# Whole products and masked evacuations in RWKV's triangular inverse, and a planner with the trace's durations

## The chip, the cores and the metric

The kernel runs on one core of one Trainium2 chip. The metric is the device time of one execution in microseconds, the median of several runs; less is better. TensorE (PE in the profile) multiplies, with a weight load (PEld) ahead of each product; VectorE (DVE), ScalarE (ACT) and GpSimd (POOL) do the elementwise work; SyncE (SP) issues the transfers.

## What is computed

One layer of a streaming encoder over 1024 prompt tokens and 32 tokens of a sample, width 1024, in float32. After an RMS norm a combined projection feeds two mixers side by side, four HGRN2 heads of 128 and eight RWKV-7 heads of 64; then come an output projection, cross attention to 256 memory rows and a SwiGLU block with 2816 hidden features.

```python
def layer(x, mk, mv, hg_s0, rw_s0, shift0, lb, lw):
    n = rmsnorm(x, lw['norm_mix'])
    p = n @ lw['w_in']
    hg_o, hg_s = hgrn2_mixer(p[..., :HG_COLS], lb, lw['hgrn_norm'], hg_s0)
    rw_o, rw_s, rw_shift = rwkv7_mixer(p[..., HG_COLS:], shift0, rw_s0, ...)
    x = x + jnp.concatenate([hg_o, rw_o], axis=-1) @ lw['w_out']
    x = x + cross_attend(rmsnorm(x, lw['norm_cross']), mk, mv, lw['w_cq'], lw['w_co'])
    n = rmsnorm(x, lw['norm_ffn'])
    x = x + (jax.nn.silu(n @ lw['w_ff1']) * (n @ lw['w_ff3'])) @ lw['w_ff2']
    return x, hg_s, rw_s, rw_shift
...
    # in rwkv7_mixer, token by token
    def step(S, xs_t):
        r_t, w_t, k_t, v_t, kk_t, a_t = xs_t
        sa = jnp.einsum('bhvk,bhk->bhv', S, -kk_t)
        S = (S * w_t[:, :, None, :] + sa[..., None] * (kk_t * a_t)[:, :, None, :]
             + v_t[..., None] * k_t[:, :, None, :])
        return S, jnp.einsum('bhvk,bhk->bhv', S, r_t)
```

The kernel doesn't run RWKV's recurrence token by token. It takes chunks of 64 tokens. Within a chunk the updates depend on one another through a strictly lower triangular 64 x 64 matrix A, and the chunk is solved with the inverse of I - A.

## The kernel before

**A recorded graph and a planner.** No engine call is issued where it stands in the code. Each call becomes a node of a graph (`Graph.record`), whose edges are the reads and writes of the tiles; products that follow one another without a `cut` share a node. `Graph.order` then runs a list schedule in time: each engine has a clock and a list of ready nodes, the most urgent node that fits is taken, and each node gets a place in SBUF or a PSUM bank for as long as it needs it. Urgency is the longest path to the end, lowered by a bias: the projections carry 1e5 less, so they fill in where the mixers' chains have nothing ready. `price` gives the microseconds of a call on its engine, `wait` the delay from one engine's result to another's use, `change` what PE loses between two nodes. The order that comes out is fixed: every engine works through its queue in it, and waits on semaphores where an operand isn't there yet. So the prices set the order, not the time of any instruction. All instructions are issued at one line (L337), and the profile is read by tiles and shapes.

**Places.** SBUF is given out in units of 66 words. Tiles in "r" regions are float32r operands; "f0", "ma", "mb" hold the rest. `FIFO` limits how many tiles of a class are live and takes them in order of recording; `AHEAD` allows two RWKV units ("rw", "rc") and one HGRN2 unit at a time; `LEAD` opens a later stage when so many nodes of the earlier ones are left.

**Stages.** Phase 0 holds the projections and the mixers, phase 1 the memory's keys and values, then output projection, cross attention, feed-forward. Large products are split in a high and a low float32r part and done as three products of 352 columns each (`gemm`).

**RWKV.** `rwkv(j)` handles a pair of heads, j = 0 to 3, in five segments: four of 256 prompt tokens (four chunks, `nc_` = 4) and the sample's 32 (one chunk). Each segment calls `inverse` once, 20 times in all. `inverse` holds A - I of both heads as the two diagonal blocks of a 128 x 128 float32 tile (`abd`) per chunk, and a float16 copy of it (`a16`). It grows the inverse by blocks of 2, 4, .. 64 in five levels after a first one, and ends with a Newton step. x is the inverse found so far and y its transpose, both stacked (128 rows of both heads, 64 columns per chunk). `product(left, right)` multiplies a block-diagonal operand with a stacked one, one product of 64 columns per chunk. Since the stationary operand has to be block-diagonal, `place` copies a stacked result into the diagonal blocks of `xbd` or `pbd`, by two ScalarE copies, one for each head. A level is then: p = a16 times y, masked by VectorE; p placed in pbd; y plus the product of xbd and p, by VectorE; x plus the product of pbd and x, by VectorE; x placed in xbd. The tiles off the diagonal are set to zero once at the start, in two sets (`DIAG` = 2) that take turns.

Of the kernel before, what the change touches and what calls it, by code (L numbers as in the profile page):

```python
# [11 lines left out]
F32 = mybir.dt.float32  # L12
F32R = mybir.dt.float32r
F16 = mybir.dt.float16
# [6 lines left out]
T = TP + NS  # L21
# [5 lines left out]
LAST = [(256, 512), (768, 288), (0, 256)]    # the tokens' blocks in the last products  # L27
# [36 lines left out]
FIFO = {"wr": 2, "wh": 2, "wl": 2, "p": 44, "h": 12, "rp": 5, "wr2": 4, "wh2": 8, "wl2": 8, "ckv": 7, "mrow": 2}  # L64
# [22 lines left out]
class View:  # L87
    """A part of a tile: the indices it covers, and the steps that make the same part of the placed tile."""
# [37 lines left out]
    def free(self):  # L126
        """The indices along the free dims."""
        return (self.ix[0] & ((1 << 20) - 1)).ravel()


class Buf:
# [24 lines left out]
    def touch(self, node, view, write):  # L156
        """Edges from the earlier accesses that this one must follow."""
# [41 lines left out]

def wait(a, b):  # L200
    """us from an engine's result to another engine's use of it."""
    if a == b:
        return 0.0
    if b == "tensor":
        return 0.2 + WAIT_PE
    return {"tensor": 0.2, "gpsimd": 0.08}.get(a, 0.14) + WAIT


def price(eng, method, args, kw):
    """(us on the engine, us until its result can be used beyond that)."""  # L210
    out = args[0] if args else kw.get("out")
    n = math.prod(out.shape[1:]) if out is not None and hasattr(out, "shape") else 1
    if method == "dma_start":
        return 0.45 + n * out.shape[0] * 4 / 380e3, 1.2
    if eng == "tensor":
        if method == "transpose":
            return (0.056 if args[1].shape[0] == 64 else 0.109), 0.0
        lhs = kw["lhsT"]
        m = math.prod(lhs.shape[1:])
        if lhs.dtype == F16:  # L220
            return 0.029, 0.0
        if lhs.dtype == F32R:
            return (n if n >= 256 else 4 * n) / 2400 + 0.002, 0.0
        return (n / 790 if m == 64 else 4 * n / 2400 + 0.003), 0.0
    if eng == "vector":
        if method == "tensor_reduce":
            n = math.prod(args[1].shape[1:])
        return 0.065 + n * 1.04e-3 + (0.065 if method in ("scalar_tensor_tensor", "tensor_tensor_scan") else 0.0), 0.0
    if method == "affine_select":
        return 0.3, 0.0  # L230
    if method == "memset":
        return 0.04 + n * 0.5e-3, 0.0
# [11 lines left out]
def change(a, b):  # L244
    """us that the tensor engine loses between two nodes' products: weights that a short product doesn't hide."""
    if a is None:
        return 0.0
# [1356 lines left out]
```

## Time and profile before

| | |
|---|---|
| median of 3 runs | 2035.69 us (2035.36 to 2036.48) |
| span of the profiled execution | 2034.7 us |
| PE busy | 1954.2 us, 96% |
| DVE, ACT, POOL busy | 1101.1, 801.0, 622.5 us |
| transfers | 100.59 MB, mean 49 GB/s |

The span runs from the first to the last instruction of one execution; what lies around it makes up the rest of a run's time. PE's busy time counts a product from its start to its modelled end, and products overlap, so a busy PE isn't one at its peak. Idle time is put down to the engine whose work ended last before the waiting instruction; "issue" stands for time in which nothing that the profile shows was waited for. Tiles go by the region of SBUF that they lie in ("f", "r", "ma", "mb", "wr") or by "bank".

### The profile page before, as it was taken

The numbers are of one execution on the slowest core, as the hardware profiler recorded it, in microseconds if no ns is written. First come the engines' busy times: TensorE is split into PE (matmuls) and PEld (weight loads), VectorE is DVE, ScalarE is ACT, GpSimd is POOL, SyncE is SP. The second block draws the span as 40 slices with busy tenths as digits, with TensorE's granted clock in tenths as the row PEclk, the third lists the DMA queues.
The fourth block names the chain that finished last, engine by engine and source line by source line (L and its number), as shares of the span: only waits on it lengthen the run. The fifth ranks groups of instructions, "written<-read, shape, count | busy, mean of one in ns | idle before, by whom it ended". The sixth has DMA issues, their size and how long they took to land.

```text
span 2034.7 us, 36538 instructions
## 1 busy us (share of the span) xinstructions
PE 1954.2 (96%) x14417; PEld 1813.2 (89%) x14417; DVE 1101.1 (54%) x2584; ACT 801.0 (39%) x2066; POOL 622.5 (31%) x954
## 2 busy tenths in 40 slices
PE   7989999998999899899999999999999999999998
PEld 6878777787877788899989999999999999999997
DVE  4876677768767766635754356333333344323345
ACT  4576546845765676633332233121111112111122
POOL 4742343334434331206300056230022233310221
PEclk8999999998999999899999999999999999999999
DMA  4100100011010101541211111111211111111112
GB/s 139 42 22 25 35 23 27 23 34 33 22 32 18 33 23 58 179 147 42 73 42 42 42 53 42 42 40 40 59 50 39 40 58 42 50 40 53 46 42 86
DMA packets 159115, 100.59 MB, mean 49 GB/s; under 512 B 7776, under 2 KB 153824, under 8 KB 158944
## 3 DMA queue, kind: packets, MB, share of 16 engines
q1 hardware_dynamic: 158944, 98.26, 16.0%
q8 instruction: 113, 1.85, 0.4%
q14 instruction: 58, 0.48, 0.1%
HBM read 86.69 MB, written 11.55 MB: 48 GB/s over the span
## 4 chain that ended last, share of the span: by engine, by line
PE 59%; DVE 4%; POOL 1%; ACT 1%; issue 1%; DMA 1%; SPq 0%; DVEq 0%; ACTq 0%
PE bank L337 59%; DVE f L337 2%; ACT f L337 1%; POOL f L337 1%; DVE r L337 1%; POOL r L337 1%; DVE mb L337 0%; ACT mb L337 0%; DMA wr<-in_w_ck_dram 0%; ACT r L337 0%; DMA f<-mix_scratch 0%; DMA wr<-in_w_cq_dram 0%; DVE wr L337 0%; SPq L337 0%; POOL mb L337 0%
## 5 line engine op out<-in xcount | busy, mean ns | idle before, releaser
L337 PE MATMUL bank<-r 128*128 128x352 f32 x5904 | 1040.1, 331 | 12.4 <-POOL r L337 5.3
L337 PEld LDWEIGHTS bank<-r 128*128 128x128 f32 x5904 | 955.1, 190 | 27.6 <-POOL r L337 5.8
L337 DVE TENSOR_TENSOR f<-bank,f 128x256 f16<-128x256 f32 (+9 forms) x689 | 252.6, 391 | 355.4 <-PE bank L337 339.8
L337 PE MATMUL bank<-mb,r 128*128 128x352 f32 (+3 forms) x2448 | 411.5, 325 | 4.6 <-DVE r L337 2.5
L337 PEld LDWEIGHTS bank<-mb,r 128*128 128x128 f32 x2448 | 396.1, 188 | 9.5 <-DVE r L337 4.3
L337 POOL TENSOR_TENSOR f<-f 128x352 f32<-128x352 f32 (+6 forms) x242 | 198.2, 835 | 482.0 <-ACT f L337 459.4
L337 PE MATMUL bank<-f 128*128 128x64 f16 (+7 forms) x2612 | 291.6, 253 | 35.2 <-DVE f L337 15.7
L337 ACT CAST r<-wr 128x1024 fp32r<-128x1024 f32 (+2 forms) x154 | 145.1, 946 | 311.8 <-PE bank L337 298.1
L337 ACT ACTIVATE f<-f 128x256 f32<-128x256 f32 (+5 forms) x372 | 147.0, 411 | 245.9 <-DVE f L337 217.7
L337 PEld LDWEIGHTS bank<-f 128*128 128x128 f32 (+4 forms) x1564 | 163.6, 162 | 66.8 <-DVE f L337 16.9
L337 ACT COPY f<-f 64x256 f16<-64x256 f16 (+1 forms) x408 | 149.1, 367 | 46.1 <-DVE f L337 37.8
L337 DVE TENSOR_TENSOR r<-wr,r 128x1024 fp32r<-128x1024 f32 (+2 forms) x124 | 142.1, 1150 | 43.5 <-ACT r L337 43.3
L337 DVE TENSOR_TENSOR wr<-wr,f 128x1024 f32<-128x1024 f32 x82 | 105.8, 1292 | 104.5 <-DMA wr<-in_w_ff_dram 89.1
L337 POOL TENSOR_TENSOR r<-f,r 128x352 fp32r<-128x352 f32 x48 | 62.3, 1312 | 271.1 <-DVE f L337 216.9
L337 POOL TENSOR_SCALAR f<-f 128x64 f32<-128x64 f32 (+6 forms) x124 | 54.7, 442 | 159.2 <-DVE f L337 100.0
L337 DVE TENSOR_TENSOR ma<-bank,ma 128x352 f32<-128x352 f32 (+6 forms) x96 | 45.3, 486 | 94.6 <-PE bank L337 84.1
L337 PEld LDWEIGHTS <-f 128*128 128x128 f16 x1156 | 52.5, 99 | 35.6 <-issue 8.2
L337 POOL TENSOR_TENSOR r<-wr,r 128x1024 fp32r<-128x1024 f32 x30 | 71.7, 2393 | 29.5 <-ACT r L337 25.9
L337 ACT CAST mb<-f 128x352 fp32r<-128x352 f32 x66 | 30.9, 484 | 123.0 <-DVE f L337 114.7
L337 PE MATMUL bank<-f,mb 64*64 64x64 f32 (+7 forms) x830 | 75.3, 250 | 1.4 <-DVE f L337 1.1
L337 ACT ACTIVATE f<-bank,f 128x256 f32<-128x256 f32 (+4 forms) x122 | 51.1, 432 | 56.4 <-DVE f L337 19.7
L337 DVE TENSOR_TENSOR f<-bank,r 128x352 f32<-128x352 f32 x60 | 30.4, 518 | 77.0 <-PE bank L337 77.0
(167 smaller groups left out, 1770.6 us busy)
## 6 DMA issues: line engine op xcount, KB each, us to landing
wr<-in_w_ff_dram SPq DMA_DIRECT2D x44, 512.0 KB
wr<-in_w_in_dram SPq DMA_DIRECT2D x30, 512.0 KB
wr<-in_w_ff_dram SPq DMA_DIRECT2D x24, 384.0 KB
f<-mix_scratch SPq DMA_DIRECT2D x24, 176.0 KB
mb<-in_x_prompt_dram SPq DMA_DIRECT2D x16, 256.0 KB
wr<-in_w_ck_dram SPq DMA_DIRECT2D x8, 512.0 KB
wr<-in_w_cv_dram SPq DMA_DIRECT2D x8, 512.0 KB
wr<-in_w_out_dram SPq DMA_DIRECT2D x8, 512.0 KB
```

Source lines behind the costliest of these rows:

```text
L337: getattr(eng, method)(*args, **kw)
```

## The change

In `inverse`, the masks of the levels become block-diagonal and have the identity taken off, so that a masked product with A - I gives p + I directly. `place` is now one VectorE operation that reads the stacked product once for each half (a broadcast over the two column blocks), multiplies it by such a mask and writes all 512 columns, zeros included. With p + I in pbd, y and x need no addition: y becomes a plain product of xbd and pbd, copied from PSUM by ScalarE, and x a product of pbd and x. Where the right operand is block-diagonal too, `product_diag` takes its two column blocks in two products that accumulate. `a16`, `xbd` and `pbd` are no longer kept in sets that take turns, but are given out for each inverse; their memsets at the start are gone.

In the planner, `price`, `wait` and `change` get other constants and cases. Two classes, "raw" and "mixed", tiles of the RWKV projections, are limited to four live ones. A node's tiles are now tried largest first and all together, and small tiles keep out of the last whole page of 16 units unless the node is the oldest one. Comments are removed.

```diff
-WAIT, WAIT_PE, SWITCH = 0.0, 0.1, 0.06
+SWITCH = 0.095
...
-FIFO = {"wr": 2, ..., "ckv": 7, "mrow": 2}
+FIFO = {"wr": 2, ..., "ckv": 7, "mrow": 2, "raw": 4, "mixed": 4}
...
+WAIT = {("vector", "tensor"): 0.2, ("vector", "gpsimd"): 0.18, "vector": 0.115, ("scalar", "tensor"): 0.1,
+        ("scalar", "gpsimd"): 0.05, "scalar": 0.02, ("gpsimd", "tensor"): 0.08, "gpsimd": 0.0, "tensor": 0.21,
+        ("sync", "tensor"): 0.08, "sync": 0.0}
 def wait(a, b):
-    if a == b:
-        return 0.0
-    if b == "tensor":
-        return 0.2 + WAIT_PE
-    return {"tensor": 0.2, "gpsimd": 0.08}.get(a, 0.14) + WAIT
+    return 0.0 if a == b else WAIT.get((a, b), WAIT[a])
 def price(eng, method, args, kw):
     if method == "dma_start":
-        return 0.45 + n * out.shape[0] * 4 / 380e3, 1.2
+        return max(0.4, n * out.shape[0] * 4 / 200e3), 1.9
...
         if lhs.dtype == F16:
-            return 0.029, 0.0
+            return max(0.029, n / 2400 + 0.002), 0.0
         if lhs.dtype == F32R:
-            return (n if n >= 256 else 4 * n) / 2400 + 0.002, 0.0
-        return (n / 790 if m == 64 else 4 * n / 2400 + 0.003), 0.0
+            return (n if n >= 256 else 4 * n) * 0.4375e-3 + 0.007, 0.0
+        if k <= 64 and m <= 64:
+            return max(0.03, n * 0.92e-3), 0.0
+        if k <= 64:
+            return max(0.112, n * 1.25e-3), 0.0
+        if m <= 64:
+            return (0.059 if n >= 64 else 0.112), 0.0
+        return max(0.223, n / 600 + 0.005), 0.0
...
     if eng == "scalar":
-        return 0.095 + n * 0.83e-3 + (0.06 if any(isinstance(kw.get(k), View) for k in ("scale", "accum_out")) else 0.0), 0.0
+        pointer = any(isinstance(kw.get(k), View) for k in ("scale", "bias", "accum_out"))
+        return (0.18 if args[1].buf.space == "PS" else 0.21) + n * 0.83e-3 + (0.095 if pointer else 0.0), 0.0
...
     if method == "tensor_tensor":
-        return 0.1 + n * 2.1e-3 + (0.45 if args[3] == ALU.pow else 0.0), 0.0
+        return 0.22 + n * 2.2e-3 + (0.45 if args[3] == ALU.pow else 0.0), 0.0
...
+def cut_of_array(call):
+    method, args, kw = call
+    op = args[1] if method == "transpose" else kw["lhsT"]
+    return op.shape[0] <= 64, method != "transpose" and math.prod(op.shape[1:]) <= 64
 def change(a, b):
...
-    return 0.033 if half else SWITCH
+    return SWITCH if a is not None and cut_of_array(a.calls[-1]) != cut_of_array(b.calls[0]) else 0.0
...
+                if not first and b.kind == "F" and b.cls not in HOME and (idle == 16).sum() < 2:
+                    cand = np.where(idle[:, None] == 16, BIG, cand)
...
+                for b in sorted(sb, key=lambda b: -b.units):
+                    at = place(b, start, first)
+                    if at is None:
+                        break
...
+        both = self.both = c.tile([128, 2, 64], F32, name="both")
+        nc.vector.tensor_copy(both.rearrange("p h u -> p (h u)"), j64)
+        def diagonal(m):
+            d = c.tile([128, 2, 64], F32, name="levd")
+            nc.vector.tensor_tensor(d, m.unsqueeze(1).to_broadcast([128, 2, 64]), both, ALU.mult)
+            return d
...
-            self.lev.append(m)
+            nc.vector.tensor_tensor(m, m, self.i64, ALU.subtract)
+            self.lev.append(diagonal(m) if l else m)
...
-            self.diag.append([self.sp.tile([128, 4, 128], dt, name=n) for n, dt in (("abd", F32), ("a16", F16), ("xbd", F16), ("pbd", F16))])
-            for t in self.diag[-1]:
-                nc.gpsimd.memset(t, 0.0)
+            self.diag.append(self.sp.tile([128, 4, 128], F32, name="abd"))
+            nc.gpsimd.memset(self.diag[-1], 0.0)
...
-        abd, a16, xbd, pbd = self.diag[self.diag_n % DIAG]
+        abd = self.diag[self.diag_n % DIAG]
         self.diag_n += 1
+        a16, xbd, pbd = (self.tmp([128, 4, 128], t, F16) for t in ("a16", "xbd", "pbd"))
...
-        def place(dst, src):
-            for hf in half:
-                S.copy(dst[hf, :nc_, hf], src[hf])
+        def product_diag(left, right):
+            ps = stacked()
+            for c in range(nc_):
+                PE.matmul(ps[:, c], lhsT=left[:, c], rhs=right[:, c, 0:64], start=True, stop=False)
+                PE.matmul(ps[:, c], lhsT=left[:, c], rhs=right[:, c, 64:128], start=False, stop=True)
+            nc.cut()
+            return ps
+        def place(dst, ps, mask):
+            V.tensor_tensor(dst[:, :nc_].rearrange("p c (h u) -> p c h u", h=2),
+                            ps.unsqueeze(2).to_broadcast([128, nc_, 2, 64]),
+                            mask.unsqueeze(1).to_broadcast([128, nc_, 2, 64]), ALU.mult)
...
-        for hf in half:
-            S.copy(a16[hf, :nc_, hf], abd[hf, :nc_, hf])
-            G.tensor_tensor(x[hf], abd[hf, :nc_, hf], bc(self.lev0x[hf]), ALU.mult)
-        place(xbd, x)
+        S.copy(a16[:, :nc_], abd[:, :nc_])
+        G.tensor_tensor(xbd[:, :nc_], abd[:, :nc_], bc(self.lev0x), ALU.mult)
         V.tensor_tensor(y, product(a16, bc(self.i16)), bc(self.lev0y), ALU.mult)
         for l in range(1, 6):
-            V.tensor_tensor(p, product(a16, y), bc(self.lev[l]), ALU.mult)
-            place(pbd, p)
-            V.tensor_tensor(y32 if l == 5 else y, product(xbd, p), y, ALU.add)
-            V.tensor_tensor(x, product(pbd, x), x, ALU.add)
-            place(xbd, x)
+            place(pbd, product(a16, y), self.lev[l])
+            S.copy(y32 if l == 5 else y, product_diag(xbd, pbd))
+            ps = product(pbd, x) if l > 1 else product_diag(pbd, xbd)
+            place(xbd, ps, self.both)
+            if l < 5:
+                S.copy(x, ps)
         V.tensor_tensor(p, product(abd, y32), bc(self.i64), ALU.add)
         V.tensor_tensor(y1, product(xbd, p), y32, ALU.add)
         return y1
```

More of the change, by code (lines that the diff above doesn't have):

```diff
@@ L63 @@
 TASTE = [{"f0": 0.0, "wr": 0.0, "r0": 0.0, "mb": 20.0, "ma": 10.0}, {"f0": 20.0, "wr": 0.0, "r0": 0.0, "mb": 0.0, "ma": 10.0}]
-FIFO = {"wr": 2, "wh": 2, "wl": 2, "p": 44, "h": 12, "rp": 5, "wr2": 4, "wh2": 8, "wl2": 8, "ckv": 7, "mrow": 2}
+FIFO = {"wr": 2, "wh": 2, "wl": 2, "p": 44, "h": 12, "rp": 5, "wr2": 4, "wh2": 8, "wl2": 8, "ckv": 7, "mrow": 2, "raw": 4, "mixed": 4}
 INDEX = (np.arange(128, dtype=np.int64)[:, None] << 20) + np.arange(8 * 1056, dtype=np.int64)[None]
@@ L227, in price @@
             n = math.prod(args[1].shape[1:])
[L228 to L232, printed above, removed]
+        if method == "tensor_tensor_scan":
+            return 0.07 + n * 2.08e-3, 0.0
+        return 0.065 + n * 1.05e-3 + (0.065 if method == "scalar_tensor_tensor" else 0.0), 0.0
     if method == "preload_act_table_set":
@@ L235, in price @@
     if eng == "scalar":
-        return 0.095 + n * 0.83e-3 + (0.06 if any(isinstance(kw.get(k), View) for k in ("scale", "accum_out")) else 0.0), 0.0
+        pointer = any(isinstance(kw.get(k), View) for k in ("scale", "bias", "accum_out"))
+        return (0.18 if args[1].buf.space == "PS" else 0.21) + n * 0.83e-3 + (0.095 if pointer else 0.0), 0.0
+    if method == "affine_select":
+        return 0.35, 0.0
+    if method == "memset":
+        return 0.06 + n * 0.5e-3, 0.0
     if method == "tensor_tensor":
-        return 0.1 + n * 2.1e-3 + (0.45 if args[3] == ALU.pow else 0.0), 0.0
+        return 0.22 + n * 2.2e-3 + (0.45 if args[3] == ALU.pow else 0.0), 0.0
     if method == "tensor_scalar":
-        return 0.2 + n * (2.6e-3 if args[4] == ALU.max else 1.1e-3), 0.0
-    return 0.1 + n * 1e-3, 0.0
-def change(a, b):
-    if a is None:
-        return 0.0
-    (_, x, kx), (m, y, ky) = a.calls[-1], b.calls[0]
-    if m == "transpose":
-        full, half = y[1].dtype == F32, False
-    else:
-        full = ky["lhsT"].dtype != F16
-        half = math.prod(ky["lhsT"].shape[1:]) == 64
-    if math.prod(x[0].shape[1:]) > 64 or not full:
-        return 0.003
-    return 0.033 if half else SWITCH
+        return 0.3 + n * (2.9e-3 if args[4] == ALU.max else 1.3e-3), 0.0
+    return 0.24 + n * 1e-3, 0.0
+def cut_of_array(call):
+    method, args, kw = call
+    op = args[1] if method == "transpose" else kw["lhsT"]
+    return op.shape[0] <= 64, method != "transpose" and math.prod(op.shape[1:]) <= 64
+def change(a, b):
+    return SWITCH if a is not None and cut_of_array(a.calls[-1]) != cut_of_array(b.calls[0]) else 0.0
 class Graph:
@@ L433, in order, with place @@
         done, oldest, out = set(), 0, []
-        def place(b, start):
+        def place(b, start, first):
             units = b.units
@@ L484, in fits @@
                     return None
-                for b in sb:
-                    if b.at is None:
-                        at = place(b, start)
-                        if at is None:
-                            return None
-                        start = max(start, at[1])
+                tried = []
+                for b in sorted(sb, key=lambda b: -b.units):
+                    at = place(b, start, first)
+                    if at is None:
+                        break
+                    start = max(start, at[1])
+                    lo, hi = at[0], at[0] + b.units
+                    tried.append((lo, hi, freed[lo:hi].copy()))
+                    freed[lo:hi] = BIG
+                for lo, hi, was in reversed(tried):
+                    freed[lo:hi] = was
+                if len(tried) < len(sb):
+                    return None
             return start
@@ L499, in take @@
                     continue
-                got = place(b, start)
+                got = place(b, start, n.i == oldest)
                 assert got is not None, "no place for " + b.name
@@ L627, in constants @@
             B = 1 << l
-            m = c.tile([128, 64], F32, name=f"lev{l}")
+            m = c.tile([128, 64], F32, tag="lev0", name="lev") if l else c.tile([128, 64], F32, name="lev0y")
             G.memset(m, 0.0)
@@ L1397, in inverse @@
         half = (slice(0, 64), slice(64, 128))
-        abd, a16, xbd, pbd = self.diag[self.diag_n % DIAG]
+        abd = self.diag[self.diag_n % DIAG]
         self.diag_n += 1
+        a16, xbd, pbd = (self.tmp([128, 4, 128], t, F16) for t in ("a16", "xbd", "pbd"))
         def bc(m):
-            return m.unsqueeze(1).to_broadcast([m.shape[0], nc_, 64])
+            return m.unsqueeze(1).to_broadcast([m.shape[0], nc_, m.shape[1]])
         def stacked():
```

19 lines of the change are left out of this document (9 added, 10 removed).

## The prediction

> **What bounds the kernel now.** I read the totals of the page first, then a table of stages cut at 890 us, where the mixers and the memory's keys end and only large products are left, then who ends the waits of the weight loads before 900 us, then the granted clock around a few gaps. Columns of the stage table: the stretch, its length, then busy time and instruction count of PE, PEld, DVE, ACT and POOL, the granted clock, the DMA share and GB/s.
>
> ```profile
> span 2034.7 us, 36538 instructions
> PE 1954.2 (96%) x14417; PEld 1813.2 (89%) x14417; DVE 1101.1 (54%) x2584; ACT 801.0 (39%) x2066; POOL 622.5 (31%) x954
> core 0: 2034.7 us, clock 0.978
> ```
>
> ```profile
> 0.00:50.00 50.00, 36.17 (x210) 33.21 (x210) 19.88 (x35) 24.42 (x63) 24.10 (x74) 0.90 0.43 141
> 0.00:890.00 890.00, 823.01 (x7492) 704.46 (x7493) 607.42 (x1716) 548.17 (x1555) 338.97 (x680) 0.95 0.16 50
> 890.00:2034.70 1144.70, 1131.17 (x6927) 1108.74 (x6925) 493.65 (x868) 252.87 (x512) 283.49 (x274) 1.00 0.17 49
> 98.00:212.00 114.00, 107.58 (x1115) 90.59 (x1114) 80.00 (x236) 82.34 (x229) 41.35 (x83) 0.97 0.08 22
> 212.00:300.00 88.00, 82.95 (x662) 69.58 (x660) 59.20 (x170) 39.37 (x125) 36.80 (x74) 0.92 0.11 32
> 1255.00:2009.00 754.00, 753.97 (x4664) 751.56 (x4664) 285.52 (x439) 133.20 (x232) 169.79 (x157) 1.00 0.15 44
> 2009.00:2034.70 25.70, 17.35 (x129) 15.08 (x127) 17.14 (x32) 8.02 (x26) 8.21 (x27) 0.88 0.45 169
> ```
>
> From 890 us on PE idles 1144.7 - 1131.2 = 13.5 us, most of it in the last 26; the feed-forward stage is 4664 products in 754.0 us, 0.162 us each, without a gap. Nothing in the change touches that work. What can move lies ahead of 890: **67.0 us of PE idle** (890 - 823.0), 13.8 of them in the first 50 us, where data first arrive, and **a clock loss**: the mean clock of 0.978 is (1 - 0.978) x 2034.7 = 45 us lost, the tail at 0.88 holds 3 of it, and the rest, about 41, lies in the first 890 at 0.95. Work on PE is otherwise the bound: any product added there is paid. In the burst 98 to 212, where inverses run, ACT (72%) and DVE (70%) are about as loaded as each other; in 212 to 300, without them, ACT falls to 45%.
>
> ```profile
> PEld bank L337 <- issue: 33.6, 111, 4.5
> PEld bank L337 <- DVE f L337: 24.1, 42, 3.4
> PEld bank L337 <- ACT f L337: 9.1, 20, 2.4
> PEld bank L337 <- ACT mb L337: 9.0, 12, 2.1
> PEld bank L337 <- POOL f L337: 8.0, 5, 6.8
> PEld bank L337 <- DVE mb L337: 6.5, 12, 3.5
> PEld bank L337 <- POOL r L337: 5.8, 2, 5.3
> PEld bank L337 <- DVE ma L337: 5.3, 10, 2.2
> PEld bank L337 <- ACT ma L337: 4.3, 8, 1.3
> ```
>
> These are the waits of PE's weight loads before 900 us (total, times, longest): DVE ends 35.9 us, ACT 22.4, POOL 13.8. "Issue" is 33.6 us in 111 pieces of 0.3, PE's own pauses, which I don't count as reachable.
>
> ```profile
> 324.00:328.00 4.00, 4.00 (x34) 3.26 (x33) 2.29 (x5) 3.14 (x9) 2.68 (x3) 1.00 0.10 24
> 332.20:335.60 3.40, 2.21 (x28) 1.60 (x26) 3.30 (x8) 1.13 (x4) 2.49 (x3) 0.99 0.00 0
> 335.60:342.40 6.80, 6.75 (x36) 5.69 (x36) 3.72 (x14) 1.82 (x5) 2.09 (x4) 0.50 0.01 2
> 461.90:465.30 3.40, 1.47 (x12) 1.03 (x11) 3.33 (x7) 0.24 (x1) 1.87 (x1) 0.99 0.02 5
> 465.30:472.10 6.80, 6.80 (x24) 5.73 (x24) 3.61 (x11) 2.93 (x8) 2.36 (x6) 0.50 0.34 100
> ```
>
> So a gap is paid twice. Behind 3.4 us in which PE was busy for 2.21 or 1.47, the clock stands at 0.50 for 6.8 us, and that costs 3.4 us where PE is wanted; 41 us is about twelve such spells.
>
> **The change part by part.** The rows of the inverse, and what its new operations resemble:
>
> ```profile
> L337 ACT COPY f<-f 64x256 f16<-64x256 f16 x320 | 128.0, 402 | 37.1 <-DVE f L337 30.2 <-POOL f L337 1.4
> L337 ACT COPY f<-ma 64x256 f16<-64x256 f16 x32 | 12.9, 402 | 0.6
> L337 ACT CAST f<-mb 64x256 f16<-64x256 f32 x32 | 12.9, 403 | 30.4 <-POOL f L337 15.5 <-DVE mb L337 14.2
> L337 ACT COPY f<-f 64x64 f16<-64x64 f16 x88 | 21.1, 240 | 9.1 <-DVE f L337 7.6 <-POOL f L337 0.2
> L337 ACT COPY f<-bank 128x256 f32<-128x256 f32 x68 | 24.3, 371 | 34.0 <-PE bank L337 27.6 <-DVE mb L337 4.2 <-DVE f L337 1.3
> L337 ACT ACTIVATE mb<-mb 128x512 f32<-128x512 f32 x16 | 10.1, 634 | 3.0 <-POOL f L337 3.0
> L337 DVE TENSOR_TENSOR f<-bank,f 128x256 f16<-128x256 f32 x229 | 90.1, 418 | 32.2 <-PE bank L337 26.5 <-ACT f L337 3.6 <-ACT mb L337 0.8
> L337 DVE TENSOR_TENSOR f<-bank,f 128x64 f16<-128x64 f32 x64 | 13.2, 218 | 8.7 <-PE bank L337 7.4 <-ACT ma L337 0.9 <-issue 0.2
> L337 DVE TENSOR_TENSOR r<-bank,r 128x512 fp32r<-128x512 f32 x16 | 10.9, 691 | 14.9 <-ACT r L337 14.9
> L337 POOL TENSOR_TENSOR f<-mb,f 64x256 f16<-64x256 f32 x30 | 21.3, 709 | 31.7 <-DVE mb L337 27.1 <-PE bank L337 3.3
> L337 POOL TENSOR_TENSOR r<-wr,r 128x1024 fp32r<-128x1024 f32 x30 | 71.7, 2393 | 29.5 <-ACT r L337 25.9 <-PE bank L337 3.2
> L337 PE MATMUL bank<-f 128*128 128x64 f16 x1048 | 72.3, 195 | 9.8 <-DVE f L337 3.7 <-ACT f L337 2.6 <-ACT mb L337 2.3
> 324.93 0.18 PEld L337 LDWEIGHTS <-f 128*128 128x128 f16 x4
> 330.52 0.29 PEld L337 LDWEIGHTS <-f 128*128 128x128 f16 x8
> ```
>
> The copy counts fix the number of inverses: 352 copies of 64x256 at 22 each are 16 whole ones, 88 of 64x64 are 4 of the sample (one chunk), 68 chunks in all.
>
> *PE.* Each level's y product becomes two per chunk, and so does the first x product: 6 more per chunk, 6 x 68 = **408 more f16 products**. From a group of 4 (0.18 us) to one of 8 (0.29) each costs 0.0275 us, so 408 cost **+11.2 us**. Bounds: 0 where they fall into idle time, +28 at the 0.069 us of the whole group of such products (72.3/1048), gaps included. I take +11: PE is the bound.
>
> *ACT.* Gone are 128.0 + 12.9 + 12.9 + 21.1 = 175 us of copies. New in a whole inverse: one copy of 512 columns (0.634) and nine from PSUM (0.371), 3.97 us, 64 us for 16; the four small ones, ten copies each at under 0.24, under 10. **ACT loses about 101 us** of its 548. What hid the old copies was filler on PE; where it did not, ACT ended the wait. If the copies were behind half of ACT's 22.4 us, **-11 us**; the ends are 0 (the waits belong to other ACT work) and -22. This cover has a successor: the evacuations on DVE are late next.
>
> *DVE.* Gone: 16 x 15 evacuations of 0.418 and 4 x 15 of 0.218, 113 us. New: 16 x 10 of 512 columns at 0.691 and 4 x 10 of 128, between 0.218 and 0.418, say 0.3: 123 us. **+9 us of work**, most beside PE; at DVE's share of reachable idle (35.9 of 607) it is +1 us, all of it on the path +9. I take +1. Some dozen mask products at the start lie in the first 50 us, where DVE is busy 19.9: 0.
>
> *POOL.* 32 operations of 0.709 become 16 of 512 columns at half of 2.393, 1.2 us: -3 us, beside other work. The memsets of six tiles go as well: 0.
>
> *Latency.* In the old loop y waits for xbd, xbd for the x product and two pairs of copies: over two levels 0.42 (y) + 0.42 (p) + 0.80 + 0.42 (x) + 0.80 = 2.86 us of evacuation and three product hops. The new loop is 0.69 + 0.37 per level, 2.12 per two levels with four hops. One hop is about 0.2 (a product takes 0.195) and a hand-over. So the chain alone hardly shortens; what falls is the number of instructions that queue, seven to four per level. I count nothing beyond the ACT term.
>
> *The planner.* Before, it took 0.149 us for a 352-column product (0.162 in the row above) and 0.31 for a copy of 64x256 (0.402); now 0.161 and 0.42. A product placed by too fast prices stands in PE's queue before its operand is there, and what stands behind it waits too. Better prices should move filler ahead of it. Nothing in the trace prices this; nearest is the idle that DVE and POOL end, 35.9 + 13.8 = 49.7. A fifth gives **-10 us**; the ends are -30 and, as any new order can also hit a gap, +15. The limits of four "raw" and four "mixed" tiles, and pages kept whole, lie within these ends: 0 extra, as three live blocks cover evacuation. DMA issues are the same; SP's queue, sorted by dearer loads (2.6 against 1.8 us by the planner), is within the same ends.
>
> *The clock.* Idle would go from 67 to about 47 (13.8 of both at the start, so 53 to 33, by 38%). Of 41 us, 5 belong to the start and some to the stage's end; 38% of the 32 or so left is **-12 us**; ends 0 and -25.
>
> A rule of the Trainium skill speaks against the last term. In "TensorE: Matmul & The Clock Gate", section "Why this matters for your kernels", it asks for no PE-idle gaps of over about 3 us. By that rule, gaps of 1 us would turn no clock down, and thinning them would save no spell. Here spells came behind windows that were 65% and 43% busy (2.21 and 1.47 of 3.40), so the trace goes with the looser reading, but it does not show how much less idle is enough.
>
> Sum: +11 - 11 + 1 - 10 - 12 = **-21 us** on the span of 2034.7; the median of the runs lies 1.0 above it, so 2034.7 + 1.0 - 21 = **2015 us**.
>
> **The rivals.**
>
> *The spells stay.* The mixers' many small products leave PE lightly used whatever the order, and about as many spells come. For it: both windows above are short of PE work, not empty. Against: 324 to 328, full of the same mix, has clock 1.00. Without the clock term: 2035.7 - 9 = **2027**. The Trainium skill's rule above, on the page named there, would have it so too.
>
> *The products are paid and nothing comes back* (slower). If ACT's waits belong to other copies, and the order is as good as before, PE has 408 more products in a row that waits as before: +11 + 1, **2048**. It decides once relief and order together return less than 12 us. For it: ACT ends only 22 us of the waits, and bursts keep PE at 94% (107.58 of 114). Against: 42 of the named waits are under 3.5 us long, the size of a queue of copies.
>
> *DVE becomes late.* Each level now has two evacuations of 0.691 in one queue in place of 0.418: 200 x 0.27 = 54 us of chain. A quarter uncovered is +14, two more spells +7, products +11, **2067** without the relief. For: DVE ends most waits already. Against: its total grows by 9 us only.
>
> *The stage closes up.* Idle before 890 halves again beyond the forecast, order -25, clock -20, ACT -11: with +12, -44, **1991**. For: the burst of 98 to 212 runs at 94% already with its waits. Against: the waits that POOL ends, 13.8, have another cause.
>
> *It doesn't do what it says*: if planner limits undo the relief, it shows as the second rival.
>
> **How the numbers follow.** Chances: forecast 0.35, spells stay 0.20, paid for nothing 0.20, DVE late 0.10, closes up 0.15. The forecast's own range is 2003 to 2030. For 8 in 10 I leave out half of the DVE case and the far side of the last: 1988 to 2052. A measurement of this kernel can tell about 0.2%, 4 us, from no change. Faster than 2031.6: 0.15 + 0.34 and half or more of the second, 0.60; within: 0.12; slower: 0.28, the two slow rivals less a little.
>
> **What would show it.** ACT before 890 near 447 us; f16 products up from 17 x 68 = 1156 to 1564; DVE evacuations of 512 columns near 0.69; PE idle there near 47; mean clock near 0.984. The stage should end near 870, and everything from there on take the same 1145 us. Idle kept with ACT's waits gone and DVE's grown is the DVE rival; idle down at an unchanged clock, the first; a stage that ends past 895, the second. It is wrong altogether if the stages after it change length by more than 5 us.

## The result, and the profile after

| | before | after |
|---|---|---|
| median of the runs | 2035.91 us (2035.36 to 2036.48) | 2056.01 us (2052.03 to 2058.04) |
| span of the profiled execution | 2034.7 us | 2054.7 us |
| ACT, DVE, POOL busy | 801.0, 1101.1, 622.5 us | 691.8, 1121.6, 614.0 us |

The changed kernel is **slower by 20 us** by these medians, 0.99%; the ratio given with the result is 1.0111, 95% interval 1.0087 to 1.0135, and before took 2031.5 to 2033.7 in the later sessions, so the loss is 20 to 25 us. The forecast was 2015 us, with 2052 as the upper end of its range. The totals of the page of the changed kernel, and its core's clock:

```profile
span 2054.7 us, 36974 instructions
PE 1961.8 (95%) x14825; PEld 1822.8 (89%) x14825; DVE 1121.6 (55%) x2496; ACT 691.8 (34%) x1784; POOL 614.0 (30%) x928
core 0: 2054.7 us, clock 0.979
```

PE has the 408 products more (14825 against 14417) and is busy for 7.6 us more; it idles 92.9 us in place of 80.5; the clock is the same within 0.001. ACT has lost 109 us of work, as meant. So the work went where it should, and the time didn't follow.

**Where the time lies.** The load of the output projection's weights, `wr<-in_w_out_dram`, opens the rest of the kernel; it waits in the weights' fifo behind the loads of the memory's keys and values. Three rows of the timeline from 700 to 1000 us of each kernel give the memory's products, that first load and the mixers' last write (shortest, median and longest of one in ns, then from the first start to the last). Before:

```profile
L337 PE MATMUL bank<-r,ma x384: 275/281/561, 804.1 to 880.6; 128*128 128x256 f32 x192
L337 SPq DMA_DIRECT2D wr<-in_w_out_dram x8: 368/390/557, 873.8 to 942.3; - x8
L337 SPq DMA_DIRECT2D mix_scratch<-f x11: 319/327/349, 708.9 to 878.1; - x11
```

After:

```profile
L344 PE MATMUL bank<-r,ma x384: 277/281/557, 816.2 to 905.3; 128*128 128x256 f32 x192
L344 SPq DMA_DIRECT2D wr<-in_w_out_dram x8: 367/390/391, 899.8 to 963.6; - x8
L344 SPq DMA_DIRECT2D mix_scratch<-f x10: 319/336/356, 742.2 to 868.1; - x10
```

The mixers end 10 us **earlier** than before. But the memory's keys and values start 12 us later and end 25 later, and the load that opens the rest comes 26.0 later. The stage tables cut there (columns as in the prediction), before:

```profile
0.00:800.00 800.00, 742.00 (x6916) 628.81 (x6917) 553.30 (x1593) 492.58 (x1417) 322.95 (x644) 0.96 0.12 36
0.00:873.80 873.80, 808.90 (x7397) 691.52 (x7398) 602.05 (x1709) 541.38 (x1542) 337.44 (x678) 0.95 0.15 47
873.80:2034.70 1160.90, 1145.28 (x7021) 1121.68 (x7021) 499.02 (x875) 259.66 (x524) 285.02 (x276) 1.00 0.17 51
```

After:

```profile
0.00:800.00 800.00, 742.32 (x7268) 633.68 (x7269) 576.13 (x1494) 376.79 (x1115) 315.15 (x617) 0.96 0.12 36
0.00:890.00 890.00, 815.09 (x7762) 697.80 (x7762) 629.50 (x1627) 432.09 (x1267) 331.08 (x654) 0.95 0.15 46
0.00:899.80 899.80, 823.06 (x7811) 705.16 (x7811) 632.99 (x1629) 435.87 (x1272) 331.08 (x654) 0.95 0.16 48
899.80:2054.70 1154.90, 1138.73 (x7015) 1117.68 (x7015) 488.58 (x867) 255.96 (x513) 282.92 (x274) 1.00 0.17 50
```

Behind the load the two kernels take 1160.9 and 1154.9 us, so all of the loss is ahead of it. Of the 26.0 us there, 11.8 are more idle of PE (64.9 to 76.7) and 14.2 more busy time (808.90 to 823.06). Most of the busy time is the 408 added products, as an experiment below shows; where the 6.0 us behind the load come from wasn't traced. Up to 800 us PE idles 58.0 and 57.7 us at the same clock of 0.96: with 116 us less of ACT work there (492.58 to 376.79) its idle time is the same. From 800 us to the load PE idles 6.9 us before (73.8 - 66.9) and 19.1 after (99.8 - 80.7).

The waits of PE's weight loads before 900 us, after (the dots stand for a row of "issue" on loads that name no bank):

```profile
PEld bank L344 <- issue: 36.7, 110, 2.9
PEld bank L344 <- DVE f L344: 31.6, 47, 4.8
PEld bank L344 <- ACT f L344: 14.8, 27, 2.0
PEld bank L344 <- ACT r L344: 11.8, 9, 6.7
PEld bank L344 <- DVE r L344: 9.5, 9, 1.9
PEld bank L344 <- DVE ma L344: 7.6, 16, 1.6
PEld bank L344 <- POOL f L344: 7.1, 2, 6.7
...
PEld bank L344 <- DVE mb L344: 4.5, 10, 1.0
PEld bank L344 <- ACT mb L344: 3.1, 4, 2.0
```

The waits that ACT ends on "f" have risen from 9.1 to 14.8, those on "mb" have fallen from 9.0 to 3.1. DVE ends 31.6 us on "f" in place of 24.1. Two rows are new among the large ones: ACT r and DVE r, 21.3 us, the splits of weights. Over half of that stands ahead of the key and value products, as the group of their weight loads shows (behind the last bar the idle ahead of them, and who ended it; before, then after):

```profile
L337 PEld LDWEIGHTS bank<-r,ma 128*128 128x128 f32 x384 | 49.9, 201 | 1.7 <-DVE r L337 1.1 <-ACT r L337 0.2 <-ACT f L337 0.2
L344 PEld LDWEIGHTS bank<-r,ma 128*128 128x128 f32 x384 | 50.5, 201 | 13.6 <-DVE r L344 7.1 <-ACT r L344 4.3 <-DVE ma L344 1.7
```

How it comes about is in the chain of work that ended last (start, length, what; its part from 852 to 877 us, without the pieces of 0.02 us):

```profile
851.96 3.95 DMA wr<-in_w_ck_dram
855.95 0.04 issue
855.99 1.06 ACT r L344
857.07 1.24 DVE r L344
858.31 0.04 issue
858.35 10.06 PE bank L344 x74
868.44 0.59 ACT f L344
869.03 0.96 ACT r L344
870.00 1.24 DVE r L344
871.24 0.04 issue
871.28 5.80 PE bank L344 x47
```

A weight arrives, ACT takes its high part (1.06), DVE its low part (1.24), and PE waits for both. While the mixers run, their products can cover this, and in before, where the mixers' last write (878.1) comes with the end of these products (880.6), the same group idles 1.7 us in all. In the changed kernel the mixers have run out at 868, and the products of the keys and values go on alone to 905.

### The profile page after: what moved, and what is told of

Read it like the earlier page. It is cut to its first block, busy times and chain, and to the rows that moved or that the text cites. A ratio compares the mean times of both kernels' runs of the same rounds, so it can differ in the third digit from the quotient of the medians.

```text
span 2054.7 us, 36974 instructions
## 1 busy us (share of the span) xinstructions
PE 1961.8 (95%) x14825; PEld 1822.8 (89%) x14825; DVE 1121.6 (55%) x2496; ACT 691.8 (34%) x1784; POOL 614.0 (30%) x928
## 4 chain that ended last, share of the span: by engine, by line
PE 59%; DVE 2%; POOL 1%; ACT 1%; DMA 1%; issue 0%; DVEq 0%; SPq 0%; ACTq 0%; POOLq 0%
PE bank L344 59%; DVE f L344 2%; POOL r L344 1%; POOL f L344 1%; DVE r L344 1%; ACT r L344 0%; ACT f L344 0%; DMA wr<-in_w_out_dram 0%; DMA wr<-in_w_ck_dram 0%; DMA f<-in_mem_prompt_dram 0%; DVE ma L344 0%; ACT ma L344 0%; DVEq L1637 0%; DVE mb L344 0%; SPq L344 0%
## 5 line engine op out<-in xcount | busy, mean ns | idle before, releaser
L344 DVE TENSOR_TENSOR f<-bank,f 128x352 f32<-128x352 f32 (+9 forms) x588 | 247.5, 445 | 328.6 <-PE bank L344 315.7
L344 POOL TENSOR_TENSOR f<-f 128x352 f32<-128x352 f32 (+7 forms) x248 | 199.5, 822 | 485.7 <-ACT f L344 454.6
L344 PE MATMUL bank<-f 64*64 64x64 f32 (+8 forms) x2526 | 283.1, 259 | 45.8 <-DVE f L344 25.6
L344 ACT ACTIVATE f<-f 128x256 f32<-128x256 f32 (+6 forms) x420 | 165.1, 408 | 261.9 <-DVE f L344 218.1
L344 PEld LDWEIGHTS bank<-f 64*64 64x64 f32 (+4 forms) x1713 | 171.4, 160 | 83.7 <-DVE f L344 27.0
L344 PE MATMUL bank<-f,mb 64*64 64x64 f32 (+9 forms) x994 | 88.1, 249 | 2.7 <-DVE f L344 2.1
L344 DVE TENSOR_TENSOR ma<-bank,f 128x512 f16<-128x512 f32 (+6 forms) x135 | 65.2, 494 | 41.8 <-PE bank L344 40.7
L344 PEld LDWEIGHTS bank<-f,mb 128*64 128x64 f32 (+6 forms) x970 | 67.4, 149 | 20.2 <-issue 8.7
L344 ACT ACTIVATE f<-bank,f 128x256 f32<-128x256 f32 (+3 forms) x133 | 54.8, 428 | 81.7 <-PE bank L344 37.2
L344 ACT CAST f<-bank 128x256 f16<-128x256 f32 (+1 forms) x148 | 48.3, 338 | 80.3 <-PE bank L344 38.6
```

The source lines that it names most:

```text
L344: getattr(eng, method)(*args, **kw)
```

## The experiments

My first theory after the result, **late filler**: the instructions are as good as forecast, but the order that the planner made of them leaves the keys and values to the end. The rivals: the 408 products, the new inverse's own chain, or the new prices lose the time in any order. A third view came with the second group of runs, **the order is a draw**. All runs in one table; "load" is the first load of the output projection's weights in the profiled execution, "idle" and "clock" are PE's ahead of it. The half-memory kernels have no such entries, since their load doesn't mark the end of the same work.

| kernel | median us | ratio to before [95%] | load at | idle | clock |
|---|---|---|---|---|---|
| before | 2031.5 to 2035.9 | | 873.8 | 64.9 | 0.95 |
| after | 2056.0 | 1.0111 [1.0087, 1.0135] | 899.8 | 76.7 | 0.95 |
| inverse_only | 2064.4 | 1.0142 [1.0120, 1.0164] | 902.5 | 82.4 | 0.95 |
| planner_only | 2080.0 | 1.0226 [1.0211, 1.0241] | 919.6 | 86.0 | 0.92 |
| before_order_a | 2064.5 | 1.0153 [1.0133, 1.0173] | 902.3 | 84.7 | 0.94 |
| before_order_b | 2049.4 | 1.0082 [1.0067, 1.0097] | 888.9 | 74.0 | 0.94 |
| after_other_order | 2041.5 | 1.0045 [1.0029, 1.0061] | 880.4 | 64.2 | 0.96 |
| rows_first | 2052.4 | 1.0089 [1.0074, 1.0104] | 893.8 | 79.9 | 0.95 |
| before_rows_first | 2034.7 | 1.0013 [1.0003, 1.0023] | 869.5 | 67.7 | 0.96 |
| fewer_products | 2052.0 | 1.0098 [1.0078, 1.0119] | 895.4 | 77.7 | 0.94 |
| before_half_kv | 2013.4 | 0.9898 [0.9873, 0.9923] | | | |
| after_half_kv | 2022.0 | 0.9932 [0.9910, 0.9954] | | | |
| order_a_half_kv | 2033.1 | 1.0003 [0.9986, 1.0020] | | | |
| after_order_c | 2022.1 | 0.9946 [0.9928, 0.9965] | 864.2 | 56.6 | 0.97 |
| after_order_d | 2012.7 | 0.9897 [0.9882, 0.9912] | 855.6 | 52.9 | 0.97 |
| inverse_order_c | 2049.4 | 1.0072 [1.0057, 1.0087] | 885.6 | 67.6 | 0.96 |
| before_order_c | 2035.6 | 1.0010 [1.0000, 1.0020] | 870.3 | 63.4 | 0.97 |
| planner_order_c | 2017.6 | 0.9914 [0.9899, 0.9929] | 861.4 | 58.0 | 0.95 |
| planner_order_d | 2049.5 | 1.0072 [1.0055, 1.0089] | 890.2 | 70.3 | 0.94 |
| before_order_d | 2014.9 | 0.9913 [0.9887, 0.9939] | 857.5 | 60.5 | 0.97 |

**Each half alone.** inverse_only takes the new inverse into the planner of before:

```diff
-            V.tensor_tensor(p, product(a16, y), bc(self.lev[l]), ALU.mult)
-            place(pbd, p)
...
+            place(pbd, product(a16, y), self.lev[l])
+            S.copy(y32 if l == 5 else y, product_diag(xbd, pbd))
...
```

> The new inverse under the planner of before. Late filler (the 20 us are lost where the mixers end, because the new planner takes up the rows of the memory late, so that the products for the memory's keys and values no longer fill the mixers' last 60 us): the old planner takes them up early, so the time is near before or a little under it, 2025 to 2040. Products paid (the 408 added products are the loss): 2045 to 2056. Order worse throughout (the new prices make stalls all along the mixers): 2025 to 2040 as well, so this run doesn't tell it from late filler.

planner_only takes the new planner and keeps the old inverse:

```diff
-WAIT, WAIT_PE, SWITCH = 0.0, 0.1, 0.06
+SWITCH = 0.095
...
-            return 0.029, 0.0
+            return max(0.029, n / 2400 + 0.002), 0.0
...
```

> The old inverse under the new planner. Late filler: the memory's rows come late here too, 2050 to 2070. Products paid: 2030 to 2040, since none is added. Order worse throughout: 2050 to 2070, with PE busy less in each stretch of 100 us up to 800, not only behind it.

Measured: 2064.4 and 2080.0, both slower than the whole change (2056.0), and both above every range that was expected. The halves don't add: with the old planner the new inverse costs 29 us (by the ratio), with the new one it saves 24. The row of planner_only up to its load:

```profile
0.00:919.60 919.60, 833.61 (x7403) 711.85 (x7403) 607.66 (x1717) 547.81 (x1551) 345.20 (x680) 0.92 0.16 47
```

It does the same work as before's 7397 products there, with no instruction of another kind, 45.8 us later: 21 us more idle (86.0 against 64.9), and 24.7 us more busy time at a clock of 0.92 against 0.95. The new planner alone gave the worst order of all. (It is the prices together with the limits and the rule for places; they weren't taken apart.)

**Other orders of the same instructions.** FREE_PS and FREE_SB are the microseconds after a tile's last use at which the planner takes its PSUM bank, or its place in SBUF, for free. They are 0.2 and 0.2 in both kernels; no instruction depends on them.

```diff
-FREE_PS, FREE_SB = 0.2, 0.2
+FREE_PS, FREE_SB = 0.262, 0.14
```

> The kernel before, unchanged but for two of the planner's constants, the time after which it takes a PSUM bank and a place in SBUF for free (0.2 and 0.2 us, here 0.262 and 0.14). They change no instruction, only the order. Lost order (the order of before is a lucky draw, any other touch of the planner or the graph loses some 20 us): 2045 to 2070, with the first load of the output projection's weights later by what the time is longer. Products paid or worse prices: 2030 to 2038.

before_order_b has 0.299 and 0.278 there, and after_other_order 0.144 and 0.227 in the changed kernel:

> The same with 0.299 and 0.278. Lost order: 2045 to 2070. Products paid or worse prices: 2030 to 2038.

> The changed kernel with the same two constants at 0.144 and 0.227, the order that the planner itself holds for the best of 24 (19 us shorter by its own reckoning than the changed kernel's). Lost order: 2032 to 2045. Products paid: 2052 to 2058, since every order holds the same products.

Measured: before loses 32 and 17 us, the changed kernel gains 15, all as "lost order" has it. So a tenth of a microsecond or less in such a constant moves either kernel by about as much as the whole change did.

**The memory's rows early.** In both kernels the rows' transposes, which the keys and values need, get the highest urgency:

```diff
+        late, nc.bias = nc.bias, -BIAS
         rs = self.load_rows(...)
+        nc.bias = late
```

> The changed kernel with one edit: the loading and transposing of the memory's rows gets the highest urgency in place of the lowest, nothing else. Late filler: the first products for the memory's keys move from 816 us to under 790, the stage ends some 15 us sooner, 2035 to 2045. Products paid or order worse throughout: 2052 to 2058, unchanged.

> The kernel before with the same edit. Late filler: its first such product comes at 804 us and its idle from 790 to 890 is 9 us, so a gain of 0 to 10 us is open to it, 2026 to 2036. Products paid or order worse throughout: 2034 to 2037.

Measured: 2052.4 (from 2056.0) and 2034.7 (ratio 1.0013 [1.0003, 1.0023]). In rows_first the last of the rows is loaded at 771.0 us in place of 833.8, yet the first product for the keys starts at 821.4 in place of 816.2, where late filler had expected it under 790. The load comes 6 and 4 us earlier, and the time hardly moves. The transposes weren't what the keys and values waited for.

**The products.** The second product of each pair is left out, with the order held: the node keeps its price and its reads.

```diff
-                PE.matmul(ps[:, c], lhsT=left[:, c], rhs=right[:, c, 0:64], start=True, stop=False)
-                PE.matmul(ps[:, c], lhsT=left[:, c], rhs=right[:, c, 64:128], start=False, stop=True)
+                node = PE.matmul(ps[:, c], lhsT=left[:, c], rhs=right[:, c, 0:64], start=True, stop=True)
+                right[:, c, 64:128].buf.touch(node, right[:, c, 64:128], False)
+                node.cost += price("tensor", "matmul", (ps[:, c],), {"lhsT": left[:, c]})[0]
```

> The changed kernel without the second of each pair of products where both operands are block-diagonal (408 products; the second head's part is left out of y and of the first x), with the planner charged for them as before, so that every instruction else stands in the same order. Products paid: 408 x 0.0275 us less, 2043 to 2047. Lost order: the same 2043 to 2047 if PE is the bound all along, 2050 to 2056 if most of them stand in time that is lost anyway.

Measured: 2052.0, 4 us less than after, the load 4.4 us earlier. The other engines' instructions come in the same order. Up to the load PE is busy for 5.4 us less than after's 823.06:

```profile
0.00:895.40 895.40, 817.66 (x7402) 698.93 (x7402) 631.56 (x1629) 434.90 (x1272) 330.90 (x654) 0.94 0.16 48
```

That isn't the price of the 408 products. The clock stood lower here, 0.94 against 0.95, and other products took longer: the group of 2160 of 352 columns on "r" is busy for 431.0 us, in after for 428.0. The groups of float16 products up to the load, added up, are busy for 97.8 us in after and 85.3 here: 12.5 us, 0.031 each, with some overlap counted in. Two runs here had a clock of 0.978, that of after's run of 2058.0; they took 2050.9 and 2049.8, 7 to 8 us less. So the added products take some 11 to 12 us of PE, as "products paid" has it, and without them 4 to 8 us come back, not the whole 20.

**Half of the memory.** To ask late filler directly (a product's `stop` is moved along with it):

```diff
-                for a in range(2):
+                for a in range(1):
                     hi, lo = self.load_w(self.i[key][0, 512 * a:...], 4, m=256, eng=nc.vector)
```

> The kernel of before with only the first half of the inner dimension in the memory's keys and values: 192 of the 384 products of 128x256 and 8 of the 16 weight loads of that stage are left out (about 192 x 0.115 = 22 us of PE). Three kernels with this edit run together: before, after, and before with the other two planner constants (the first slower order). Theory A, late filler: a slower order is slower because the key and value products start late and then stand alone, paced by their weights, ahead of the load that opens the rest; before had them nearly hidden, so it gains the least, at most the 22 us of work: 2012 to 2022. Theory B, an order worse throughout (idle and turned-down clock all through the mixers): every one of the three gains the same, here 2010 to 2022.

> The same edit in the changed kernel (192 of the 384 products for the memory's keys and values and 8 of the 16 loads left out). Theory A: the mixers of this order end some 10 us ahead of those of before and only the key and value products hold the next stage back, so it gains 30 to 40 us, and its difference to before_half_kv is within 8 us (it was 20). Theory B: the difference stays 15 to 25 us, 2030 to 2045.

> The same edit in the kernel of before with planner constants 0.262 and 0.14 (32 us slower than before with all of its products; mixers' last write 11 us ahead of before's). Theory A: difference to before_half_kv within 10 us. Theory B: 25 to 35 us stay.

Measured: 2013.4, 2022.0 and 2033.1. Before gains 20 us, about the work taken out; the changed kernel 34; the slow order of before 31. Against before_half_kv 8.6 us of the changed kernel's 20 stay, and 19.7 of the slow order's 32. So late filler accounts for some 12 us in each, over half of the loss in the one and well under half in the other, and **not for the rest**. In the slow order the rest is clear of theory A's bound of 10. In the changed kernel 8.6 us are too near the bound of 8 to decide, since the intervals of the two kernels overlap. The planner made a new order in each of the three, so this split is no finer than the spread of orders.

**Orders that are chosen.** Since neither view had asked what the change is worth in a good order, I had the planner make some 300 orders of the changed kernel, by moving four things that change no instruction: the two constants, from which count of nodes on the keys and values may open, and their bias, with and without the rows early. The shortest by the planner's own sum of prices were run, and likewise of the others.

```diff
-FREE_PS, FREE_SB = 0.2, 0.2
+FREE_PS, FREE_SB = 0.188, 0.143
...
-LEAD = {0: BIG, 1: 1100, 2: 250, 3: 400, 4: 300, 5: 40}
+LEAD = {0: BIG, 1: 1500, 2: 250, 3: 400, 4: 300, 5: 40}
...
-        nc.phase, nc.bias = 1, 2 * BIAS
+        nc.phase, nc.bias = 1, 0.0
```

This is after_order_d; the others have their own values in the same places, and before_order_c, before_order_d, planner_order_c and planner_order_d have the memory's rows early as well.

> The changed kernel in another order: FREE_PS, FREE_SB = 0.174, 0.186, the key and value stage opens with 1300 nodes left in place of 1100 and with a bias of BIAS / 2 in place of 2 * BIAS, so that its products are taken earlier (the planner reckons 27.9 us less than for the changed kernel's own order; its other order reckoned 18.7 less and gained 15 on the chip). No instruction differs. Theory A, the order is what was lost: 2028 to 2040, level with before. Theory B, the changed instructions cost it whatever the order: 2045 or more. Rival C, the forecast was right but for the order: under 2025.

> The changed kernel in a third other order: 0.188, 0.143, opening at 1500 nodes left, bias 0 (reckoned 26.8 us less). Theory A: 2028 to 2042. B: 2045 or more. C: under 2025.

> The new inverse with the planner of before, in the shortest order of some 170: 0.144, 0.187, opening at 1500, bias BIAS / 2 (reckoned 7.3 us less than inverse_only, which took 2064). Theory A: as reckoned orders of the planner of before go on the chip (before 1774 reckoned and 2034, first other order some 15 to 25 more on the chip), 2040 to 2055. B, the products cost it whatever the order: 2055 or more. C: under 2030.

> The kernel of before in the shortest order of some 170: 0.217, 0.191, opening at 1300, the memory's rows transposed early (reckoned 3.3 us less than before). If the order of before is already about the best that such a search finds, 2028 to 2040; under 2020 would say that before had much left to win by order alone, and over 2045 that the reckoning doesn't carry to the chip.

(The search of before held 109 orders by then, not the 170 that its expectation gives.)

Measured: 2022.1 and **2012.7**, rival C in both; 2049.4; 2035.6. The changed instructions can run 1% faster than before, 43 us faster than in the order that they came with. The rows of after_order_d, timeline and stage:

```profile
L344 PE MATMUL bank<-r,ma x384: 275/281/468, 770.7 to 861.2; 128*128 128x256 f32 x192
L344 SPq DMA_DIRECT2D wr<-in_w_out_dram x8: 367/386/391, 855.6 to 918.6; - x8
L344 SPq DMA_DIRECT2D mix_scratch<-f x10: 319/327/377, 722.8 to 851.5; - x10
```

```profile
0.00:855.60 855.60, 802.73 (x7810) 693.05 (x7810) 621.21 (x1622) 433.08 (x1265) 335.28 (x654) 0.97 0.16 48
855.60:2011.60 1156.00, 1139.73 (x7015) 1118.25 (x7015) 491.83 (x874) 259.41 (x520) 281.49 (x274) 1.00 0.18 52
```

It does after's 7811 products (7810 here) in 44.2 us less: 23.9 us of idle less (76.7 to 52.9) and 20.3 of busy time. The clock accounts for most of the second: a loss of (1 - 0.95) x 899.8 = 45 us against (1 - 0.97) x 855.6 = 26 with these rounded shares, 42.7 against 25.6 by the trace's own record of the clock. The keys and values start 45 us earlier, 81 us ahead of the mixers' end, and run among the mixers; but the mixers too end 17 us earlier. Both parts of the order matter, as the half-memory runs had it. The wait ahead of the key and value products isn't the whole of it: it is 13.6 us in after and 5.4 here, but 3.5 and 4.9 in inverse_order_c and planner_order_d, which both took 2049.

At this point the change looked good and badly ordered. Two questions remained: which half carries the gain, and whether before gains as well when as many of its orders are tried.

> The old inverse under the new planner, in the shortest order of some 165 by the planner's own reckoning (0.144, 0.307, opening at 900, the memory's rows transposed early; reckoned 33.7 us less than planner_only, which took 2080). If the new prices alone carry the gain of the best order of the changed kernel (2012.7), this comes to 2005 to 2022; if the new inverse carries it, or only both together do, to 2030 to 2055.

> The same with the second order of that search (0.158, 0.127, opening at 1100, rows early; reckoned 31.8 us less than planner_only). Prices alone: 2005 to 2025; the inverse, or both together: 2030 to 2060.

> The kernel of before in the shortest of 279 orders by the planner's own reckoning (109 when before_order_c was chosen, 170 more since, so that as many are tried as for the changed kernel): 0.131, 0.22, opening at 1500, bias BIAS / 2, the memory's rows transposed early (reckoned 4.8 us less than before). If before has no more to win by order, 2025 to 2045, and the best order of the changed kernel (2012.7) stays ahead; if its place ahead comes only from trying more orders, under 2020.

Measured: 2017.6, 2049.5 and **2014.9**. Before, with none of the change, is as fast in that one of its 279 orders which the planner sums up as the shortest. So the changed kernel's place ahead came from trying more orders, the second of the two readings that were expected. Its rows:

```profile
0.00:857.50 857.50, 796.97 (x7402) 680.62 (x7402) 594.71 (x1711) 542.11 (x1547) 340.19 (x680) 0.97 0.16 48
857.50:2015.70 1158.20, 1144.18 (x7015) 1121.15 (x7015) 497.24 (x875) 257.07 (x519) 283.34 (x274) 1.00 0.17 51
```

Beside after_order_d it has 5.8 us less PE work ahead of the load (796.97 against 802.73, with 408 products fewer) and 7.6 us more idle (60.5 against 52.9), with 109 us more of ACT work. So in good orders the change gains and loses about the same: the two, 2014.9 and 2012.7, have ratios with overlapping intervals. If one takes for the changed kernel too the order that the planner sums up as the shortest (after_order_c), it is 7 us behind. after_order_d and before_order_d are the fastest of the kernels that do all the work, and both beat the two that were compared.

planner_order_c and planner_order_d say how much is left to chance: their sums of prices differ by 1.9 us and their times by 32. The orders run of before span 2014.9 to 2064.5, those of the changed kernel 2012.7 to 2056.0, those of the new planner with the old inverse 2017.6 to 2080.0. A loss of 20 us is well inside each.

## Why the prediction was wrong

**The step that failed is "The planner".** It gave -10 us to a new order, because better prices should move filler ahead of late products, with -30 and +15 as ends. Measured alone on the old inverse, the new planner is worth +46 in its own order and -17 and +15 in two others, by the ratios of the table. In the changed kernel PE's idle time ahead of the load rose by 11.8 us where the whole forecast had it fall by 20. Prices nearer to the trace did not make a better order by themselves: a list schedule takes the most urgent node at each turn, and a small change sends it another way for the rest of the 900 us. With what the runs show, the term could only have been a draw, 0 with ends as far off as these, -17 and +46. Without it, and without the clock term that rested on the idle it was to save, the forecast's sum is +1, no change, and the measured +20 lies inside such ends. The -11 for ACT's relief, below, was not seen either; how much of it a better order would return stays open.

**What bounds the kernel** was right in kind: PE with its idle time and clock in the first 900 us, and a constant rest. The rest is 1160.9 and 1154.9 us from the load on; over all orders it stays within 1153 to 1162. The forecast called itself wrong altogether if this part changed by more than 5 us; cut at the load it got 6.0 shorter, so by its own sign it failed here too, if barely. The cut at 890 us, "where the mixers and the memory's keys end", tied the stage's end to the mixers. These ended at 868 as the forecast's 870 would have it, and the stage went on to 900 with keys and values.

**PE, +11**: right. There are 408 more products, as counted, and their time on PE is some 12 us by the rows (0.031 us each, against 0.0275).

**ACT, -11**: ACT's work fell by 109 us in all (801.0 to 691.8), against the 101 forecast. That PE would get 11 us of it back was not seen: its idle time up to 800 us is 58.0 before and 57.7 after. With its order chosen the new inverse has 7.6 us less idle than the old one, which may be this relief, but lies within what another order does.

**DVE, +1**: its busy time grew by 20.5 us, not 9; its operations, added one by one, take 11 us more, and the rest is that they overlap less. The new evacuations took 0.685 us, as forecast (0.691). The waits it ends rose from 24.1 to 31.6 us on "f", but they are 17.6 in after_order_d, with the same instructions, so that is the order and not the inverse:

```profile
PEld bank L344 <- DVE f L344: 17.6, 39, 3.3
```

**The clock, -12**: nothing, since no idle was saved; 0.95 in both kernels ahead of the load. The sum of the idle time doesn't set the clock by itself: after_order_d and before_order_d have 0.97 with 52.9 and 60.5 us of it, but planner_order_c has 0.95 with 58.0, and before_order_c 0.97 with 63.4. The rule of the Trainium skill in "TensorE: Matmul & The Clock Gate", section "Why this matters for your kernels", asks for no gaps of over about 3 us. The trace of before goes with the looser reading: ahead of the load its clock record has 12 spells at 0.50, and in the 3.4 us in front of 6 of them PE was busy for 44 to 71% and had no gap of 2 us.

**The rivals.** "The products are paid and nothing comes back", 2048, came nearest, with the right sign, and its mark, a stage that ends past 895 us, came true. Its term for the products held; its "the order is as good as before" did not, as the 11.8 us more of idle ahead of the load show. "DVE becomes late" had the symptom in this one order and not the cause.

What stays open: whether the new inverse is worth a few microseconds. Its effect is -24 or +29 by the planner that goes with it in the orders as they came, -2 between the best orders that were run, and +7 between those that the planner sums up as the shortest. To settle less than 5 us against a spread of 50 takes many orders of each, or one order kept by hand.

## What to carry to other kernels

Where a planner sets the order, a change of any node or price deals a new order, and two single timings compare two draws: nudge a constant that changes no instruction in both kernels first, and see by how much the time moves. Then compare the best of equally many orders of each; here that turned +20 us into level, and was worth 1% to either kernel, more than the change was. And before crediting relief on a second engine, find the load or product that opens the next stage and ask what it waits for: here it was in part filler that was left over, and not only the chain that had been relieved.

## What the hardware showed beside it

In two places of the trace of before a VectorE operation on two tiles in SBUF is held for as long as a large GpSimd operation runs. The timeline at 461 and 645 us (start, length, operation, idle ahead of it):

```profile
461.34 2.43 POOL L337 TENSOR_TENSOR r<-wr,r 128x1024 fp32r<-128x1024 f32 x1
461.49 2.56 DVE L337 TENSOR_TENSOR ma<-ma,f 128x256 f32<-128x256 f32 x1
...
644.17 0.41 DVE L337 TENSOR_TENSOR f<-f,ma 128x256 f32<-128x256 f32 x1
645.25 2.48 DVE L337 TENSOR_TENSOR f<-mb,ma 128x192 f32<-128x192 f32 x1 [0.67 <-POOL mb L337]
645.18 2.34 POOL L337 TENSOR_TENSOR r<-wr,r 128x1024 fp32r<-128x1024 f32 x1
648.41 0.97 PE L337 MATMUL bank<-mb 64*128 64x128 f32 x5 [4.25 <-DVE mb L337]
```

The two VectorE operations, of 256 and 192 columns, took 2.56 and 2.48 us, where one of 256 took 0.41, and ended 0.3 and 0.2 us after GpSimd's. PE's product behind the second came after 4.25 us of idle. Neither planner prices this, and neither did the forecast. The Trainium skill has it, in "SBUF — State Buffer", section "SBUF: two separate sides": a VectorE operation with two inputs in SBUF and a GpSimd operation that reads SBUF lock one another out for a whole instruction, and the later one waits. Both rows agree. It doesn't make the spread of orders: VectorE operations between tiles in SBUF, of up to 352 columns, that took over 1.5 us number 3 in before, 3 in after, 4 in before_order_d and 2 in after_order_d, 5 to 9 us in all. Longer operations weren't counted.
